# Splitting the even mixer's input weights during the first feed-forward instead of in the mixer

## The chip, the core and the metric

One core of a Trainium2 chip. The metric is the device time of one execution in microseconds (us). The engines are TensorE (PE, matmuls), VectorE (DVE), ScalarE (ACT), GpSimd (POOL) and SyncE (SP, which here only issues loads). SP and POOL can both issue DMA transfers; every engine takes its instructions strictly in order.

## The reference

Two layers over 256 latent and 256 context tokens of width 1024, all in float32. Layer 0 is what matters here:

```python
y = modulate(h, g, m[off], m[off + 1])                       # rmsnorm, scale, shift
h = h + 0.5 * m[off + 2] * swiglu(y, w_gu, w_down)           # half_ffn, context and latent
...
z_ctx = y_ctx @ w_in                                         # even_mixer: 1024 -> 2816
z_lat = y_lat @ w_in
f_lat = fourier_mix(z_lat[..., D_A_IN:])
r_l, v_l, kk_l, g_l, dirs_l = rwkv_features(token_shift(zA_lat, mu), *fargs)
S, y = wkv_scan(S0, ...)                                     # two directions, 12 heads
out = jnp.concatenate([o, f], axis=-1) @ w_out
```

The modulation vectors m come from c @ ada_w, a matrix-vector product of 1024 by 9216.

## The kernel before

**Products of float32 in three passes.** A weight tile of 128 columns (1024x128, 512 KB) is loaded by SP into a buffer `wraw` (4 of them). ACT casts it to the reduced format (`whi`, L190), DVE subtracts the cast from the original (`wlo`, L191), and `mm3` (L195 to L197) adds up whi·xh, whi·xl and wlo·xh on PE. In the first feed-forward whi/wlo stand in five pairs of buffers, in the mixer in four; a pair is used about four tiles after it is made.

**The first feed-forward** (`ffn`, context and latent together, 512 columns) goes over 22 blocks f in three parts: f 0 to 7, 8 to 14, 15 to 21. Each f takes two weight tiles (gate and up); then ACT makes `sg` = silu(gate), DVE multiplies it into `hd`, ACT casts `hh`, DVE subtracts `hl`. After each part comes `down`, 8 steps k, on the part's hh and hl. The last two k of the last part are done for context first, then for latent.

**Background jobs.** `net.jobs` is a list of generators; `run_jobs(n)` takes n steps of the first unfinished one before each f and each k. Before the change the jobs are the 28 `ada_job`s: POOL loads 1 MB (`adaw`, 3 buffers `ada0`), and DVE forms products with the conditioning row, with a scratch tile `adaj` (1 buffer), L281.

**The transition.** The last sums of squares go through DVE (`ms`, L347), POOL (a power, `rs`, L350) and PE (L356, spreads it over rows). DVE makes `hn`, ACT `yh` and DVE `yl` tile by tile k; POOL writes `hlat` to memory (`spill`, L1205). PE starts four weight tiles of the mixer at once, context columns first (v = 1), then latent (v = 0).

**The mixer's input part.** 22 weight tiles `win`, in the order of `win_order` (one, then six times three, then three). The first four are split at the end of the feed-forward; `even_in` splits each of the other 18 as it comes. Between them stand the `features` of the first group: token shift (`zp`, `z`), scans, the small products L631, L650 and the inverse of a triangular matrix (`Dt`, L678; L687). A scheduler that works with its own model of durations puts all instructions into each engine's order, so that a removed instruction can move others. The chain of scans follows from about 545 us on.

Of the kernel before, what the change touches and what calls it, by code (L numbers as in the profile page):

```python
# [7 lines left out]
F32 = mybir.dt.float32  # L8
F32R = mybir.dt.float32r
AF = mybir.ActivationFunctionType  # L10
ALU = mybir.AluOpType
AX = mybir.AxisListType

P = 128
D = 1024
KT = D // P
# [56 lines left out]
def win_order():  # L73
    o = [18]
    for j in range(NP):
        o += [NP + j, 2 * NP + j, j]
    return o + [19, 20, 21]
# [56 lines left out]
class Net:  # L134
# [138 lines left out]
    def ada_job(self, blk, vecs):  # L273
# [4 lines left out]
        for i in range(2):  # L278
# [3 lines left out]
                                               op1=ALU.mult, accum_out=self.mod[0, v][:, blk + i:blk + i + 1])  # L282
            yield

    def run_jobs(self, n):
        drive(self.jobs, n)

# [206 lines left out]
        self.bd = self.cst[:, C_BD:C_BD + P]  # L494

    def even_in(self, i, n, yh, yl):
        wh, wl = self.weight(self.ins["win"][i])
        tag = ("down", "mx", "down", "ada", "pg", "pg")[i % 6]
        if tag == "pg":
            if i % 2 == 0:  # L500
                self.two = self.bank("pg")
            ps = self.two[:, i % 2, :]
        else:
            ps = self.bank(tag)
        for k in range(KT):
            self.mm3(ps[:, :n], wh[:, k, :], wl[:, k, :], yh[:, k, :n], yl[:, k, :n], k == 0, k == KT - 1)
        return ps
# [601 lines left out]
def drive(gens, n):  # L1109

    while gens and n:
        if next(gens[0], gens) is gens:
            gens.pop(0)
        else:
            n -= 1


def body(tc, ins, out):
    with ExitStack() as ctx:
        nc = tc.nc  # L1120
        net = Net(ctx, tc, ins, out)
        psum = lambda name: tc.tile_pool(name=name, bufs=1, space=bass.MemoryType.PSUM)
        net.ada_setup()
        spill = tc.dram_tile([P, KT, T], F32, name="spill")
        acc = net.keep.tile([P, 2 * T], F32, name="acc")
        with ExitStack() as yp:
            ypool = yp.enter_context(tc.tile_pool(name="ey", bufs=1))
# [2 lines left out]
            op = ctx.enter_context(ExitStack())  # L1130
            mx = ExitStack()
            with tc.tile_pool(name="hc", bufs=1, side="right") as hcp, tc.tile_pool(name="f1", bufs=1) as fp:
                hc = hcp.tile([P, KT, T], F32, name="hctx")
                hl = hcp.tile([P, KT, T], F32, name="hlat")
                for q in range(4):
                    k = slice(2 * q, 2 * q + 2)
                    nc.sync.dma_start(hl[:, k, :], ins["tok"][0][:, k, :])
                    nc.sync.dma_start(hc[:, k, :], ins["tok"][1][:, k, :])
                h = [hl, hc]
                with psum("ps1") as net.pp:  # L1140
                    net.ap, net.hp = fp, ((ypool, 4),) * 4 + ((fp, 1),)
                    two = [fp.tile([P, 2, KT, 256], F32, tag=t, name="ada0" + t, bufs=1) for t in ("hh", "hl")]
                    load = [two[b // 2][:, b % 2] for b in range(4)]
                    load += [fp.tile([P, KT, 256], F32, tag="ada0", name=f"ada0{b}", bufs=3) for b in range(4, 7)]
                    load += [fp.tile([P, KT, 256], F32, tag="cb", name="ada07", bufs=1)]
                    nc.sync.dma_start(load[0], ins["ada0"][0])
                    srcs = [ins["gu"][0, f, j] for f in range(2) for j in range(2)]
                    raws = [net.load(x) for x in srcs]
                    for b in range(1, KT):
                        nc.sync.dma_start(load[b], ins["ada0"][b])  # L1150
                    yh, yl = parts2()
                    abt = fp.tile([P, 2, 2, KT], F32, name="ab0")
                    ab = [(abt[:, v, 1, :], abt[:, v, 0, :]) for v in range(2)]

                    def start():

                        first, ws = [], []

                        def begin(b):
                            if b < KT:  # L1160
                                first.append(net.ada_first(b, load[b], abt))
                                next(first[b])

                        def split():
                            ws.append(net.weight(srcs[len(ws)], 0, raws[len(ws)]))

                        def ready(k):
                            if k < KT:
                                drive([first[k]], 1)
                                net.modulate_tile(k, h, (0, 1), r, ab, yh, yl, fp)  # L1170

                        with tc.manual_schedule(engines={mybir.EngineType.PE, mybir.EngineType.DVE, mybir.EngineType.Activation}):
                            for k in range(KT):
                                for v in range(2):
                                    net.stat(acc, h[v][:, k, :], v, k)
                            rs = net.rates(net.sums(acc, (0, 1)), 4, D, NORM_EPS)
                            begin(0)
                            r = net.spread_rows(rs, 4)
                            for i in range(4):
                                if i == 1:  # L1180
                                    ready(0)
                                split()
                            begun = [net.bank("gu") for _ in ws]
                            for k in range(KT):
                                for n, (ps, (wh, wl)) in enumerate(zip(begun, ws)):
                                    net.mm3(ps, wh[:, k, :], wl[:, k, :], yh[:, k, :], yl[:, k, :], k == 0, k == KT - 1)
                                    if k and n == 0:
                                        ready(k + 1)
                                        if k == KT - 2:
                                            net.early = [net.weight(ins["gu"][0, 2, j], 0) for j in range(1)]  # L1190
                                if k == 0:
                                    begin(1)
                                    ready(1)
                                begin(k + 2)
                        return begun

                    net.jobs = [net.ada_rows_job(fp, (0, 1))]
                    net.jobs += [net.ada_job(m * KT + k, (0, 1) if m < 5 else (0,)) for m in range(2, 9) for k in range(0, KT, 2)]
                    gate = lambda: [net.modcol(0, v, 2, scale=0.5) for v in range(2)]
                    rate = {}  # L1200
                    net.between = net.rstd_steps(acc, 1, rate)
                    net.ffn(0, h, yh, yl, gate, acc, fp, 2, start)
                    net.run_jobs(100)
                ab = [(net.modcol(0, v, 4, g=net.normg(0, 1)), net.modcol(0, v, 3)) for v in range(2)]
                nc.gpsimd.dma_start(spill, hl)  # L1205
                yh, yl = parts2()
                net.pp = mx.enter_context(psum("pse"))
                net.even_params(net.keep)

                net.hp = ((ypool, 4),)  # L1210
                order = win_order()
                ws = [net.weight(ins["win"][i], 0) for i in range(4)]
                begun = [net.bank(t) for t in ("down", "down", "mx", "ada")]
                for v in (1, 0):
                    c = slice(v * T, v * T + T)
                    late = net.rstd_steps(acc, 0, rate) if v else None
                    for k in range(KT):
                        if v and k in (2, 5):
                            next(late)
                        net.modulate_tile(k, h, (v,), rate[v], ab, yh, yl, hcp)  # L1220
                        for m, ps, (wh, wl) in zip(order, begun, ws):
                            own = m < NP
                            if not (own and v):
                                net.mm3(ps[:, c], wh[:, k, :], wl[:, k, :], yh[:, k, c], yl[:, k, c],
                                        k == 0 and (own or v == 1), k == KT - 1, skip_group_check=True)
# [34 lines left out]
        with tc.tile_pool(name="late", bufs=1) as lp:  # L1260
            wide = [net.ada_wide(b, lp) for b in range(18)]
            outs = []
            for g in range(3):
# [7 lines left out]
                else:  # L1271
                    gate = net.modcol(0, 0, 5)
# [16 lines left out]
        h = [hl]  # L1289
# [3 lines left out]
        fp = ctx.enter_context(tc.tile_pool(name="post", bufs=1))  # L1293
# [72 lines left out]
```

## Time and profile before

| | |
|---|---|
| median of 3 runs | 1600.86 us (1598.47 to 1601.13) |
| the profiled execution | 1593.66 us, span in the trace 1592.0 us |
| busy in the span | PE 94%, DVE 68%, ACT 42%, POOL 13% |
| first feed-forward | to 404.8 us |
| mixer's input part with the first group's features | 404.8 to about 545 us |
| loads of `win` | 22 x 512 KB by SP, between 366.8 and 505.9 us |
| idle on POOL ahead of `rs` at 402.69 us | 194.86 us |

Shares are of the whole span. PE's busy time counts a matmul to its modelled end, so a stretch can be full while each matmul runs at half clock; the granted clock is a column of its own.

### The profile page before, as it was taken

What the parts mean: (1) busy time and instruction counts of PE and PEld (TensorE: products, weight loads), DVE (VectorE), ACT (ScalarE), POOL (GpSimd) and SP (SyncE); (2) the same over time, 40 slices, a digit from 0 to 9 for tenths busy, and PEclk for the clock granted to TensorE, in tenths of its full rate; (3) what the DMA queues carried; (4) which work ended last, traced back from release to release, by engine and by line L of the source; (5) the groups of instructions that cost most, each with busy time, mean ns of one, the idle gap of its engine ahead of it and who ended that gap; (6) DMA issues with size and microseconds to landing.
All of it is one profiled execution on the core that took longest, in us unless ns stands there. A gap on an engine that the chain in (4) does not pass through costs nothing.

```text
span 1592.0 us, 29925 instructions
## 1 busy us (share of the span) xinstructions
PE 1488.8 (94%) x12102; PEld 1279.8 (80%) x12102; DVE 1082.7 (68%) x1994; ACT 675.4 (42%) x1101; POOL 202.3 (13%) x293
## 2 busy tenths in 40 slices
PE   5999999999989979899998999999999986899997
PEld 3788888888877755455686999999999874899997
DVE  4799963334689699577266777657775399767753
ACT  3422222223454462542444555445554365445542
POOL 0000100000131151321211000000000075200000
PEclk9999999999999889999799999999999988899999
DMA  9676953232322025455432555655556432345562
GB/s 373 236 238 235 335 200 103 93 92 82 125 84 84 28 102 203 169 197 194 150 108 69 171 181 180 179 190 173 186 176 178 137 106 92 121 161 184 183 181 88
DMA packets 68810, 253.40 MB, mean 159 GB/s; under 512 B 8032, under 2 KB 10864, under 8 KB 63936
## 3 DMA queue, kind: packets, MB, share of 16 engines
q1 hardware_dynamic: 64080, 219.46, 42.0%
q0 software_dynamic: 4592, 32.03, 5.7%
q8 instruction: 95, 1.56, 0.4%
q14 instruction: 43, 0.35, 0.1%
HBM read 249.36 MB, written 2.10 MB: 158 GB/s over the span
## 4 chain that ended last, share of the span: by engine, by line
PE 80%; DVE 13%; ACT 2%; issue 2%; POOL 1%; DMA 1%; SPq 0%; POOLq 0%; DVEq 0%; ACTq 0%
PE gu L195 13%; PE gu L196 13%; PE gu L197 13%; PE down L195 7%; PE down L196 7%; PE down L197 7%; PE ada L260 3%; PE gu L970 1%; PE gu L1055 1%; DVE wlo L191 1%; DVE oo L1028 1%; DVE ocv L1028 1%; PE pg L746 1%; PE down L804 1%; PE misc L631 1%
## 5 line engine op out<-in xcount | busy, mean ns | idle before, releaser
L190 ACT CAST whi<-wraw 128x1024 fp32r<-128x1024 f32 (+1 forms) x298 | 304.6, 1026 | 524.1 <-PE gu L196 227.2
L191 DVE TENSOR_TENSOR wlo<-wraw,whi 128x1024 fp32r<-128x1024 f32 (+1 forms) x298 | 356.3, 1198 | 151.9 <-ACT whi L190 144.9
L195 PE MATMUL gu<-yh,whi 128*128 128x258 f32 (+1 forms) x1408 | 438.3, 312 | 6.2 <-ACT yh L375 4.3
L196 PE MATMUL gu<-yl,whi 128*128 128x258 f32 (+1 forms) x1408 | 437.7, 311 | 0.1
L197 PE MATMUL gu<-yh,wlo 128*128 128x258 f32 (+1 forms) x1408 | 436.8, 310 | 0.0
L195 PEld LDWEIGHTS gu<-yh,whi 128*128 128x128 f32 x1408 | 265.8, 189 | 24.1 <-ACT yh L375 5.7
L196 PEld LDWEIGHTS gu<-yl,whi 128*128 128x128 f32 x1408 | 267.2, 190 | 15.1 <-DVE yl L377 1.0
L197 PEld LDWEIGHTS gu<-yh,wlo 128*128 128x128 f32 x1408 | 267.3, 190 | 14.9 <-DVE wlo L191 0.8
L196 PE MATMUL down<-hl,whi 128*128 128x256 f32 (+1 forms) x704 | 217.3, 309 | 0.0
L195 PE MATMUL down<-hh,whi 128*128 128x256 f32 (+1 forms) x704 | 217.3, 309 | 0.0
L197 PE MATMUL down<-hh,wlo 128*128 128x256 f32 (+1 forms) x704 | 217.3, 309 | 0.0
L196 PEld LDWEIGHTS down<-hl,whi 128*128 128x128 f32 x704 | 134.4, 191 | 7.4
L195 PEld LDWEIGHTS down<-hh,whi 128*128 128x128 f32 x704 | 134.4, 191 | 7.4
L197 PEld LDWEIGHTS down<-hh,wlo 128*128 128x128 f32 x704 | 134.4, 191 | 7.4
L350 POOL TENSOR_TENSOR rs<-ms,mhalf 128x2 f32<-128x2 f32 (+1 forms) x9 | 10.9, 1208 | 821.4 <-DVE ms L347 821.4
L281 DVE SCALAR_TENSOR_TENSOR adaj<-adaw,cb 128x1024 f32<-128x1024 f32 x80 | 97.7, 1221 | 4.9 <-DMA adaw<-in_adat_dram 3.6
L260 PE MATMUL ada<-wraw,ccs 128*32 128x512 f32 x288 | 71.5, 625 | 0.7 <-DVE mod L269 0.7
L384 DVE SCALAR_TENSOR_TENSOR hlat<-down,mc,hlat 128x256 f32<-128x256 f32 x46 | 22.2, 483 | 63.0 <-PE down L197 63.0
L438 DVE COPY wb<-gu 128x1 f32<-128x1 f32 x132 | 20.2, 153 | 46.6 <-PE gu L197 46.6
L360 ACT CAST hh<-hd 128x256 fp32r<-128x256 f32 (+1 forms) x88 | 40.4, 461 | 25.0 <-DVE hd L433 14.2
L970 PE MATMUL gu<-yo,wraw 128*128 128x256 f32 x192 | 45.4, 396 | 1.9 <-ACT yo L375 1.9
L1012 POOL TENSOR_TENSOR opart<-opart,opr 128x256 f32<-128x256 f32 x54 | 44.9, 832 | 5.0 <-ACT opr L1010 1.2
(341 smaller groups left out, 2311.9 us busy)
## 6 DMA issues: line engine op xcount, KB each, us to landing
wraw<-in_gu_dram SPq DMA_DIRECT2D x176, 512.0 KB, 4.0
wraw<-in_ada_dram SPq DMA_DIRECT2D x72, 512.0 KB, 4.3
adaw<-in_adat_dram POOLq DMA_DIRECT2D x28, 1024.0 KB, 5.6
wraw<-in_down_dram SPq DMA_DIRECT2D x64, 448.0 KB, 3.3
wraw<-in_down_dram SPq DMA_DIRECT2D x32, 512.0 KB, 3.5
wraw<-in_win_dram SPq DMA_DIRECT2D x22, 512.0 KB, 3.8
wraw<-in_owin_dram SPq DMA_DIRECT2D x14, 512.0 KB, 3.6
ada<-in_ada_dram SPq DMA_DIRECT2D x4, 1024.0 KB, 16.8
```

Source lines behind the costliest of these rows:

```text
L190: nc.scalar.copy(hi[:, :k, :], raw[:, :k, :])
L191: (eng or nc.vector).tensor_tensor(out=lo[:, :k, :], in0=raw[:, :k, :], in1=hi[:, :k, :].bitcast(F32), op=ALU.subtract)
L195: mm(ps, lhsT=wh, rhs=xh, start=start, stop=False, **k)
L196: mm(ps, lhsT=wh, rhs=xl, start=False, stop=False, **k)
L197: mm(ps, lhsT=wl, rhs=xh, start=False, stop=stop, **k)
L260: nc.tensor.matmul(ps[32 * g:32 * g + 32, :], lhsT=self.cs[:, k, :], rhs=w[:, i, :], start=k < 4, stop=k >= 4, tile_position=(0, 32 * g), ...
L281: nc.vector.scalar_tensor_tensor(out=junk, in0=w[:, i, :], scalar=1.0, in1=self.cb[v], op0=ALU.mult, op1=ALU.mult, accum_out=self.mod[0, v ...
L360: self.nc.scalar.copy(hi, x)
L384: nc.vector.scalar_tensor_tensor(out=h[v][:, k, :], in0=ps[:, n * T:n * T + T], scalar=gate[v][:, k:k + 1], in1=h[v][:, k, :], op0=ALU.mul ...
L970: nc.tensor.matmul(ps[:, :n], lhsT=w[:, k, :], rhs=y[:, k, :], start=k == 0, stop=k == KT - 1)
L1012: nc.gpsimd.tensor_tensor(out=part, in0=prev, in1=pr, op=ALU.add)
L1028: nc.vector.scalar_tensor_tensor(out=c, in0=u[:, w:w + T], scalar=cw[:, j, w:w + 1], in1=c, op0=ALU.mult, op1=ALU.add)
```

## The change

Each of the 22 tiles of `win` gets a job, behind the 28 `ada_job`s: POOL loads the raw tile into the scratch tile `adaj` (1 buffer, the same that the ada products used), ACT casts it, DVE subtracts, and POOL writes both results (1 MB) to a tensor `halves[i]` in memory. The steps per f and per k go from 2 to 3. In the mixer `ready_weight` takes the place of `weight`: SP loads whi and wlo (512 KB each) straight into the pair's buffers. So 44 loads (22 MB) by SP stand where 22 (11 MB) stood, POOL issues 22 loads (11 MB) and 22 writes (22 MB) more, and the 22 casts and 22 subtractions move from the mixer and the feed-forward's end into the feed-forward.

```diff
--- before.py
+++ after.py
@@ -281,6 +281,28 @@
                 nc.vector.scalar_tensor_tensor(out=junk, in0=w[:, i, :], scalar=1.0, in1=self.cb[v], op0=ALU.mult,
                                                op1=ALU.mult, accum_out=self.mod[0, v][:, blk + i:blk + i + 1])
             yield
+
+    def halves_job(self, i):
+
+        nc = self.nc
+        raw = self.ap.tile([P, KT, P], F32, tag="adaj", name=self.nm("adaj"), bufs=1)
+        nc.gpsimd.dma_start(raw, self.ins["win"][i])
+        yield
+        w = self.ap.tile([P, 2, KT, P], F32R, tag="ada0", name=self.nm("halves"), bufs=3)
+        nc.scalar.copy(w[:, 0], raw)
+        nc.vector.tensor_tensor(out=w[:, 1], in0=raw, in1=w[:, 0].bitcast(F32), op=ALU.subtract)
+        nc.gpsimd.dma_start(self.halves[i], w.bitcast(F32))
+        yield
+
+    def ready_weight(self, i):
+
+        pool, bufs = self.hp[self.turn % len(self.hp)]
+        self.turn += 1
+        hi = pool.tile([P, KT, P], F32R, tag="whi", name=self.nm("whi"), bufs=bufs)
+        lo = pool.tile([P, KT, P], F32R, tag="wlo", name=self.nm("wlo"), bufs=bufs)
+        for q, t in enumerate((hi, lo)):
+            self.nc.sync.dma_start(t.bitcast(F32), self.halves[i][:, q])
+        return hi, lo
 
     def run_jobs(self, n):
         drive(self.jobs, n)
@@ -494,7 +516,7 @@
         self.bd = self.cst[:, C_BD:C_BD + P]
 
     def even_in(self, i, n, yh, yl):
-        wh, wl = self.weight(self.ins["win"][i])
+        wh, wl = self.ready_weight(i)
         tag = ("down", "mx", "down", "ada", "pg", "pg")[i % 6]
         if tag == "pg":
             if i % 2 == 0:
@@ -1122,6 +1144,7 @@
         psum = lambda name: tc.tile_pool(name=name, bufs=1, space=bass.MemoryType.PSUM)
         net.ada_setup()
         spill = tc.dram_tile([P, KT, T], F32, name="spill")
+        net.halves = [tc.dram_tile([P, 2, KT, P], F32, name=f"halves{i}") for i in range(len(win_order()))]
         acc = net.keep.tile([P, 2 * T], F32, name="acc")
         with ExitStack() as yp:
             ypool = yp.enter_context(tc.tile_pool(name="ey", bufs=1))
@@ -1196,10 +1219,11 @@
 
                     net.jobs = [net.ada_rows_job(fp, (0, 1))]
                     net.jobs += [net.ada_job(m * KT + k, (0, 1) if m < 5 else (0,)) for m in range(2, 9) for k in range(0, KT, 2)]
+                    net.jobs += [net.halves_job(i) for i in range(len(win_order()))]
                     gate = lambda: [net.modcol(0, v, 2, scale=0.5) for v in range(2)]
                     rate = {}
                     net.between = net.rstd_steps(acc, 1, rate)
-                    net.ffn(0, h, yh, yl, gate, acc, fp, 2, start)
+                    net.ffn(0, h, yh, yl, gate, acc, fp, 3, start)
                     net.run_jobs(100)
                 ab = [(net.modcol(0, v, 4, g=net.normg(0, 1)), net.modcol(0, v, 3)) for v in range(2)]
                 nc.gpsimd.dma_start(spill, hl)
@@ -1209,7 +1233,7 @@
 
                 net.hp = ((ypool, 4),)
                 order = win_order()
-                ws = [net.weight(ins["win"][i], 0) for i in range(4)]
+                ws = [net.ready_weight(i) for i in range(4)]
                 begun = [net.bank(t) for t in ("down", "down", "mx", "ada")]
                 for v in (1, 0):
                     c = slice(v * T, v * T + T)
```

POOL's order from the end of the feed-forward on, before: the last `adaw` loads, then `rs` of the context half, the write of `hlat`, `rs` of the latent half.

```order
L277 DMA adaw_373_2043<-in_adat_dram 128x2048
L277 DMA adaw_380_2079<-in_adat_dram 128x2048
L350 TENSOR_TENSOR rs_513_2937<-ms_512_2935,mhalf_68 128x2
L587 MEMSET ff_591_3399 128x8
L1205 DMA spill_80<-hlat_92 128x2048
L350 TENSOR_TENSOR rs_543_3057<-ms_542_3055,mhalf_68 128x2
```

After the change (`adaj` as the target of a load is a raw tile of `win`; `halvesN` on the left is tile N in memory, `halves` on the right its two parts in SBUF):

```order
L289 DMA adaj_441_2351<-in_win_dram 128x1024
L294 DMA halves19_100<-halves_452_2421 128x2048
L289 DMA adaj_453_2425<-in_win_dram 128x1024
L294 DMA halves20_101<-halves_454_2427 128x2048
L289 DMA adaj_465_2499<-in_win_dram 128x1024
L372 TENSOR_TENSOR rs_557_3091<-ms_556_3089,mhalf_68 128x2
L1229 DMA spill_80<-hlat_114 128x2048
L294 DMA halves21_102<-halves_466_2501 128x2048
L372 TENSOR_TENSOR rs_583_3203<-ms_582_3201,mhalf_68 128x2
```

The write of tile 20 and the load of raw tile 21 now stand ahead of the context half's `rs`, and the write of tile 21 ahead of the latent half's; in front of these rows the 38 others alternate in the same way from the last `adaw` on.

ACT's order at the end of part 2 of the feed-forward, before (the last `sg` and `hh` here are those of f = 14):

```order
L432 ACTIVATE sg_321_1777<-gu_316_1721 128x512
L190 CAST whi_356_1942<-wraw_358_1944 128x896
L360 CAST hh_243_1337<-hd_322_1778 128x512
L190 CAST whi_363_1978<-wraw_365_1980 128x896
L432 ACTIVATE sg_334_1851<-gu_329_1795 128x512
L190 CAST whi_370_2014<-wraw_372_2016 128x896
L360 CAST hh_243_1337<-hd_335_1852 128x512
L190 CAST whi_377_2050<-wraw_379_2052 128x896
```

And with the change, the same place:

```order
L454 ACTIVATE sg_351_1865<-gu_346_1809 128x512
L190 CAST whi_386_2042<-wraw_388_2044 128x896
L382 CAST hh_267_1407<-hd_352_1866 128x512
L292 CAST halves_354_1873<-adaj_353_1871 128x1024
L190 CAST whi_393_2080<-wraw_395_2082 128x896
L454 ACTIVATE sg_364_1941<-gu_359_1885 128x512
L190 CAST whi_400_2120<-wraw_402_2122 128x896
L382 CAST hh_267_1407<-hd_365_1942 128x512
L292 CAST halves_368_1953<-adaj_355_1877 128x1024
L190 CAST whi_407_2158<-wraw_409_2160 128x896
```

The casts of tiles 3 and 4 stand around the `sg` and `hh` of f = 14, so that these come behind the arrival of raw tile 3. The other casts stand in the same way, one in two or three of ACT's weight casts; that of tile 20 stands four rows ahead of the mixer's first `yh`, that of tile 21 between the second `yh` and the third.

SP's order at the transition, before:

```order
L181 DMA wraw_504_2849<-in_down_dram 128x896
L181 DMA wraw_525_2998<-in_win_dram 128x1024
L181 DMA wraw_528_3004<-in_win_dram 128x1024
L181 DMA wraw_531_3010<-in_win_dram 128x1024
L181 DMA wraw_534_3016<-in_win_dram 128x1024
L181 DMA wraw_584_3354<-in_win_dram 128x1024
L181 DMA wraw_607_3453<-in_win_dram 128x1024
L181 DMA wraw_613_3494<-in_win_dram 128x1024
L547 DMA up_573_3322<-in_up_dram 128x256
L845 DMA gup_1238_6917<-in_gup_dram 128x128
```

And with the change:

```order
L304 DMA whi_571_3158<-halves2_83 128x1024
L304 DMA wlo_572_3159<-halves2_83 128x1024
L304 DMA whi_573_3162<-halves3_84 128x1024
L304 DMA wlo_574_3163<-halves3_84 128x1024
L569 DMA up_613_3468<-in_up_dram 128x256
L867 DMA gup_1260_7027<-in_gup_dram 128x128
L569 DMA up_653_3669<-in_up_dram 128x256
L304 DMA whi_622_3498<-halves4_85 128x1024
L304 DMA wlo_623_3499<-halves4_85 128x1024
L304 DMA whi_644_3595<-halves5_86 128x1024
L304 DMA wlo_645_3596<-halves5_86 128x1024
```

Before, raw tiles 4, 5 and 6 are asked for ahead of `up`, and wait only for a `wraw`. Now the parts of tile 4 come behind both `up` loads, and their targets are the pair of buffers that tile 0 holds until its last matmul.

## Rows read from the trace of the kernel before

**Rows 1.** The page: busy time, share, instructions.

```profile
PE 1488.8 (94%) x12102; PEld 1279.8 (80%) x12102; DVE 1082.7 (68%) x1994; ACT 675.4 (42%) x1101; POOL 202.3 (13%) x293
```

**Rows 2.** Windows: length, busy by engine, PE clock, DMA share, GB/s.

```profile
100.00:220.00 120.00, 120.00 (x523) 97.90 (x522) 114.23 (x195) 30.99 (x36) 11.09 (x21) 1.00 0.77 276
220.00:400.00 180.00, 180.00 (x810) 147.97 (x809) 68.32 (x96) 48.52 (x67) 0.00 (x0) 1.00 0.30 95
428.00:545.00 117.00, 106.24 (x1017) 90.70 (x1016) 97.99 (x166) 59.96 (x88) 24.28 (x49) 0.91 0.26 84
```

**Rows 3.** Groups of instructions by line, 428 to 530 us.

```profile
L191 DVE TENSOR_TENSOR wlo<-wraw,whi 128x1024 fp32r<-128x1024 f32 x18 | 22.1, 1244 | 6.8 <-PE ada L196 6.4 <-ACT whi L190 0.3
L190 ACT CAST whi<-wraw 128x1024 fp32r<-128x1024 f32 x18 | 18.4, 1045 | 23.4 <-PE down L196 12.5 <-PE pg L196 8.3 <-PE ada L196 2.5
```

**Rows 4.** PE's waits, 428 to 545 us: total, times, longest.

```profile
PE misc L631 <- POOL zp L514: 3.9, 2, 3.4
PE misc L650 <- DVE bk L604: 2.5, 1, 2.5
PE misc L687 <- DVE Dt L678: 1.8, 1, 1.8
```

**Rows 5.** Timeline of all engines, 402 to 411 us: the transition.

```profile
402.45 0.16 DVE L347 TENSOR_SCALAR ms<-misc 128x2 f32<-128x2 f32 x1 [0.30 <-PE misc L335]
...
405.02 0.48 DVE L384 SCALAR_TENSOR_TENSOR hlat<-gu,mc,hlat 128x256 f32<-128x256 f32 x1 [0.83 <-PE gu L197]
...
405.80 0.59 POOL L1205 DMA_DIRECT2D spill<-hlat  x1 [0.59 <-DVE hlat L384]
...
406.71 0.50 PE L195 MATMUL down<-yh,whi 128*128 128x256 f32 x2 [1.52 <-ACT yh L375]
...
410.58 0.48 PE L195 MATMUL down<-yh,whi 128*128 128x256 f32 x2
```

**Rows 6.** The tile `cb`: its two loads (512 KB each), and their landings.

```profile
L239 POOL DMA_DIRECT2D cb<-in_crow_dram x2: 527/528/530, 54.3 to 54.8; - x2
...
DMA to landing us min/median/max: 4.3/4.7/5.0
```

**Rows 7.** DMA issues of POOL, 60 to 410 us: KB, median to landing.

```profile
spill<-hlat POOLq DMA_DIRECT2D x1, 1024.0 KB, 5.5
```

**Rows 8.** The same, 68 to 140 us.

```profile
adaw<-in_adat_dram POOLq DMA_DIRECT2D x10, 1024.0 KB, 5.1
```

**Rows 9.** The same, 192 to 209 us.

```profile
adaw<-in_adat_dram POOLq DMA_DIRECT2D x4, 1024.0 KB, 7.9
```

**Rows 10.** Timeline of DVE around the last ada product.

```profile
216.86 1.21 DVE L281 SCALAR_TENSOR_TENSOR adaj<-adaw,cb 128x1024 f32<-128x1024 f32 x1
```

**Rows 11.** Timeline, 249 to 253.6 us: the last block f of part 2.

```profile
250.02 0.62 ACT L360 CAST hh<-hd 128x512 fp32r<-128x512 f32 x1
...
253.23 0.39 PE L195 MATMUL down<-hh,whi 128*128 128x512 f32 x1
253.47 0.40 PE L196 MATMUL down<-hl,whi 128*128 128x512 f32 x1
```

**Rows 12.** Timeline of PE, 468 to 474 us: behind its longest wait.

```profile
469.03 1.98 PE L631 MATMUL misc<-cst,inv 128*64 128x128 f32 x16 [3.42 <-POOL zp L514]
...
472.39 0.63 PE L196 MATMUL pg<-yl,whi 128*128 128x512 f32 x1
472.81 0.63 PE L197 MATMUL pg<-yh,wlo 128*128 128x512 f32 x1
```

**Rows 13.** Timeline, 427 to 431 us: the first `even_in` tile.

```profile
427.66 0.28 PE L197 MATMUL down<-yh,wlo 128*128 128x256 f32 x1
...
428.96 0.50 PE L195 MATMUL pg<-yh,whi 128*128 128x512 f32 x1
...
430.22 0.50 PE L197 MATMUL pg<-yh,wlo 128*128 128x512 f32 x1 [0.53 <-DVE wlo L191]
```

**Rows 14.** The tensor `win`: landings of its 22 loads.

```profile
DMA to landing us min/median/max: 3.2/3.8/5.9
```

## The prediction

> **What bounds the kernel now.** The page comes first: PE is busy 94% of the span [rows 1], so only what PE waits for counts. The windows then split the stretch that the change touches in three [rows 2]. From 100 to 220 us PE is full (120.00 of 120) and DVE nearly so (114.23, mostly ada products). From 220 to 400 us PE is full again (180.00 of 180) while DVE does 68 us, ACT 49 and POOL nothing, and the DMA engines are busy 0.30 of the time: this is the empty room into which the jobs are put. From 428 to 545 us, the mixer's input part, PE does 106.24 of 117 us at a mean granted clock of 0.91 while DVE does 98. There 18 subtractions take 22.1 us of DVE and 18 casts 18.4 us of ACT [rows 3], and PE's three longest kinds of wait (8.2 of its 10.8 idle us) are on the features: L631 behind `zp`, L650 behind `bk`, L687 behind `Dt` [rows 4]. So the change takes work from a stretch where DVE makes PE wait and puts it where PE never waits. What it adds is latency: a chain of jobs, and a first wait of PE for loads.
>
> **The chain of jobs.** All 22 raw tiles go through `adaj`, of which there is one buffer. A raw load is issued behind the write of the tile before it, and its cast and subtraction must read it before the next may land. So one tile costs a cycle c = cast + subtraction + step to POOL + write and load. Cast 1.05, subtraction 1.24 [rows 3]; latencies on the way about 0.1; the step from DVE's end to POOL's issue, 0.3, is that from `hlat` (ends 405.50) to the write (405.80) [rows 5]. Write and load stand in no row together. Lower bound: the load overtakes the write, then only POOL's issue of the write (0.59 [rows 5]) stands before a load that lands as the two of `cb` did, 4.7 [rows 6]: 5.3. In turn: the one write of 1 MB landed 5.5 after its issue [rows 7], and of the two `cb` loads, issued 0.5 apart and landed after 4.3 and 5.0 (I read the later as the slower), the second came 1.2 behind the first [rows 6]: 6.7. Upper bound: four 1 MB loads that followed each other closely needed 7.9 where those of a quieter stretch needed 5.1 [rows 8, 9]; 7.9 behind the issue of the write is 8.5. I take 6.5, near the value in turn, because both go through one queue. So c = 9.2, between 8.0 and 11.2.
>
> The Trainium skill, "DMA: Bandwidth & Descriptors", section "Two DMAs through the same engine are not ordered", says that descriptors of one queue start in order but are pipelined; the 1.2 us between the `cb` loads agrees, and by it the load would not overtake. Its section "Anatomy of one DMA" prices a GpSimd transfer at 2.0 us plus its bytes at 436 GB/s, an estimate of 5.6 us for write and load in a row; the landings of `cb` (4.3 to 5.0 for 512 KB) lie above its 3.2.
>
> The first raw load must wait for the last ada product, which ends at 218.07 [rows 10]: issued 218.4, landed about 222.9. Cast i then comes at 222.9 + c·i, tile 20 at 406.9. Behind its subtraction (done 409.2) DVE has the last updates of `hlat` and `ms`, about 0.5, so `ms` stands at 409.7 instead of 402.45. From `ms` to the mixer's first matmul were 4.26 us (402.45 to 406.71 [rows 5]); POOL's two issues, ahead of `rs`, add 0.7 (0.3 and two times 0.59 against 0.65 for `hlat` and `ms`). PE starts the mixer at 414.7 instead of 406.71: 8.0 late. Tile 21's raw lands at 416.1, its subtraction ends at 418.4, and `yl` of k = 2 stands behind it, 418.9; PE asked for k = 2 3.9 us after its first matmul [rows 5], 418.6. That adds 0.3 to 0.5. Together D = 8.5, and 2.0 more or less for each 0.1 of c. It cannot go below about 2, since the subtraction of tile 20 (1.24) and the two issues (1.2) stand ahead of `rs` even when the chain keeps pace; that is so below c = 8.8, where cast 20 would have come at 398.9.
>
> Part of D shows earlier, and isn't added. ACT takes its casts in order, so that a late raw tile holds `hh` behind it. Cast 3 comes at 250.5; behind it stand a weight cast, `sg`, another and `hh`, some 3.7 us with the 1.05: `hh` is ready at 254.2, where before it was at 250.64 and PE asked for it at 253.23 [rows 11]. PE stalls there 1 to 2 us, and again at the end of part 3. The weight casts themselves have the lead of several buffers and are covered.
>
> **The clock.** Behind a wait of 3.42 us, PE still did matmuls of 512 columns every 0.42 us at 472.81, where elsewhere they come every 0.24 [rows 11, 12]: the lower of its two levels, 1.2 instead of 2.4 GHz, for 3.8 us or more from 469.03, of which half is lost, 1.9 or more. A start of the mixer 8 us late, of which most is one wait, I charge with 2.5, by that row a little longer; nothing, if the lateness is cut into short waits.
>
> **The first even_in.** Before, its raw tile lay ready, and PE waited 0.53 for the subtraction [rows 13]. Now its two parts go into the buffers of tile 0, whose last matmul ends at 427.94 [rows 13]. SP's loads of `win` landed after 3.2 to 5.9, median 3.8 [rows 14]: whi is there at 431.3 to 431.8, wlo a little later. PE began this tile at 428.96. So it waits 2.4 to 3.5 more, less the 0.53: 2.5. Queued behind on PE is the whole rest of the input part. Later pairs of loads have the time of a whole tile on PE (24 matmuls at 0.23 are 5.6 us for those with 512 columns) plus the lead of three other pairs, and cost nothing; without that lead each would cost the same 2.5. `up` waits for the write of tile 21 (about 424), is ahead of these loads on SP, and lands before 427.9 plus D; hidden by the context and latent halves of the first four tiles, 21 us.
>
> **More traffic.** 22 loads and writes, 34.6 MB in 180 us, are 192 GB/s beside 95: the level of 100 to 220 us, 276 GB/s at a share of 0.77, where PE didn't wait [rows 2]. I charge nothing beyond c; if SP's weight loads came too late all the same, each us would count on PE in full. Three job steps instead of two add no work and DVE was full there already: nothing, at worst a product ahead of a needed subtraction (1.2).
>
> **The gain.** 22.1 us leave DVE's 98 in the input part [rows 2, 3]. At best all 10.8 idle us go and the clock's 9% of 117 with them, 18 after what both share; at worst nothing, since the scheduler also moves the features' matmuls earlier in PE's order, so that they may be waited for as long. The three waits of 8.2 [rows 4] are on chains through DVE. I let three quarters of them go, 6, and with the longest the slow stretch behind it, 2 to 3: 9.
>
> **Sum.** 8.5 + 2.5 + 2.5 - 9 = +4.5. The profiled execution took 1593.7, which is 7.2 below the median of the runs shown (and below all three); 1598.2 in its terms is 1605 beside a median of 1600.9. A difference under 0.2%, 3.2 us, can't be told from no change.
>
> **The rivals.**
> *The chain keeps pace (faster).* If write and load overlap, c is near 8.0 to 8.6 and D is 2. No wait is then long enough to slow the clock: 2 + 2.5 - 9 = -4.5, 1596. For it: the lower bound. Against it: one queue, and the two `cb` loads. It decides below c = 9.0, where the sum is nil. By the formula of the Trainium skill, "DMA: Bandwidth & Descriptors", "Anatomy of one DMA", the estimate of 5.6 us would make c 8.3 and this the outcome.
> *The chain falls far behind.* Contention with SP's loads and the wait for DVE or ACT between other work make c 9.7 or more: D = 18 at 9.7, 25 at 10. +14 to +21: 1615 to 1622. For it: 7.9 us for close 1 MB loads, and a DMA share of about 0.8. Against: those had two megabytes in flight. The upper bound itself, 11.2, would be 40 us on top of the forecast and is left out of the range for that reason.
> *No relief in the mixer.* PE waits for the features as before, only in other places: the gain is 0 to 2 with D as forecast, about 1613. For it: the bound is latency through POOL, ACT and DVE, not DVE's load alone (L631 waits for POOL's `zp`). Against: DVE does 98 of 117 us there.
>
> **How the numbers follow.** Forecast (c 9.0 to 9.5, gain 6 to 12; 1601 to 1610): 0.42, of it 0.13 within 0.2% and 0.29 slower. Pace kept: 0.26 (0.24 faster, 0.02 same). Far behind: 0.18, slower. No relief: 0.14 (0.05 same if c is small, 0.09 slower). So faster 0.24, same 0.20, slower 0.56. The range from 1595 to 1619 leaves out the slower half of the second rival and the best of the first; the forecast's own is 1601 to 1610.
>
> **What would show it.** POOL's raw loads at even distances: 9.2 or not. ACT waiting for `adaj` ahead of its half casts; PE idle for `hh` about 253 us and 6 us or more ahead of the mixer's first matmul, with a lower clock behind it; a wait of about 3 us of the first pg matmul on a load; DVE at some 76 us in the input part, and PE's waits for `zp`, `bk` and `Dt` shorter. The prediction is wrong above all if c is off by 0.3, which moves the time by 6 us, or if the slow clock follows the late start for longer than it did in the row.

## The result, and the profile after

The changed kernel took 1610.74 us (median of 6 runs, 1608.81 to 1615.55) beside 1599.99 us for the kernel before; the ratio is 1.0070, with a 95% interval from 1.0055 to 1.0086. It is slower by 10.7 us, 8.8 to 13.8. The forecast was slower, 1605 in a range from 1595 to 1619: the sign and the range held, and the 4.5 us of its sum are less than half of what came. The profiled executions are 1593.66 before and 1608.81 after, 15 us apart; the one of before lies 6 us below its own median, and a second profile of each kernel (below) shows how much of the traces is chance.

The windows of the changed kernel stand beside those of [rows 2]: length, busy time by engine (PE, PE's weight loads, DVE, ACT, POOL), PE's clock, DMA share, GB/s.

```profile
220.00:260.00 40.00, 40.00 (x177) 32.79 (x176) 18.68 (x23) 14.90 (x18) 4.24 (x8) 1.00 0.72 255
...
340.00:380.00 40.00, 35.88 (x150) 28.64 (x149) 16.92 (x20) 14.83 (x20) 4.24 (x8) 0.96 0.66 236
380.00:420.00 40.00, 34.67 (x194) 29.97 (x193) 19.76 (x39) 11.07 (x21) 5.55 (x10) 0.96 0.79 273
...
443.71:556.70 112.99, 103.39 (x1011) 87.06 (x1011) 74.84 (x146) 40.62 (x67) 22.90 (x47) 0.94 0.48 163
```

The feed-forward, full on PE before, has holes from 340 us on. The last window is the mixer's input part, which now begins at 443.71 instead of 428.96: DVE has 75 us of work instead of 98, and yet the part is only 3.3 us shorter (116.3 from 428.96 to 545.27 before, 113.0 now).

The timeline of POOL shows the chain of jobs (start, duration, line, what, idle before and what ended it):

```profile
212.60 0.53 POOL L289 DMA_DIRECT2D adaj<-in_win_dram  x1 [10.35 <-DVE mc L314]
218.91 0.54 POOL L294 DMA_DIRECT2D halves<-halves  x1 [5.78 <-DVE halves L293]
219.43 0.54 POOL L289 DMA_DIRECT2D adaj<-in_win_dram  x1
...
390.51 0.54 POOL L294 DMA_DIRECT2D halves<-halves  x1 [8.06 <-DVE halves L293]
391.04 0.53 POOL L289 DMA_DIRECT2D adaj<-in_win_dram  x1
403.14 0.54 POOL L294 DMA_DIRECT2D halves<-halves  x1 [11.57 <-DVE halves L293]
403.67 0.53 POOL L289 DMA_DIRECT2D adaj<-in_win_dram  x1
413.59 0.54 POOL L294 DMA_DIRECT2D halves<-halves  x1 [9.39 <-DVE halves L293]
414.12 0.53 POOL L289 DMA_DIRECT2D adaj<-in_win_dram  x1
414.66 0.74 POOL L372 TENSOR_TENSOR rs<-ms,mhalf 128x2 f32<-128x2 f32 x1
```

From the write of tile 0 to that of tile 18 there are 171.60 us, 9.53 per tile: eleven cycles of 9.1 to 9.3 us and seven of 10.1 to 10.3, in which the cast begins about 7 us after its load's issue instead of 6 (why was not found). The next two cycles take 12.6 and 10.5: by then, from 390.57 us on, SP loads the first ready parts. The DMA share of 0.79 by itself does not explain it, since it was 0.82 from 260 to 300 us at cycles of 9.1 to 9.2. The `rs` that the mixer waits for stands right behind the write of tile 20 and the load of raw tile 21.

PE's waits in the changed kernel, 55 to 560 us (total, times, longest), are:

```profile
PE down L195 <- ACT hh L382: 3.9, 1, 3.9
PE misc L653 <- POOL inv L584: 3.1, 2, 2.8
PE misc L357 <- ACT sq L336: 3.0, 1, 3.0
PE pg L195 <- DMA whi<-halves: 2.7, 1, 2.7
PE pg L195 <- DVE z L540: 2.6, 2, 2.3
PE misc L709 <- DVE Dt L700: 1.3, 1, 1.3
```

Of [rows 4], the waits of L631 (now L653) and of L687 (now L709) are still there, shorter, the first now for `inv`; that for `z` is 2.6 instead of 0.9. The first, third and fourth are the price of the change. ACT's timeline shows how the first comes about:

```profile
369.64 1.04 ACT L292 CAST halves<-adaj 128x1024 fp32r<-128x1024 f32 x1 [6.33 <-DMA adaj<-in_win_dram]
370.59 0.93 ACT L190 CAST whi<-wraw 128x896 fp32r<-128x896 f32 x1
...
372.57 0.62 ACT L382 CAST hh<-hd 128x512 fp32r<-128x512 f32 x1 [1.05 <-DVE hd L455]
```

ACT stands idle for 6.3 us before a raw tile that has not landed, and the last `hh` of part 3 comes behind it, too late for PE. Over 220 to 400 us ACT waits 63.4 us in 16 such places:

```profile
ACT halves L292 <- DMA adaj<-in_win_dram: 63.4, 16, 7.7
```

At the transition it goes on, now with the sums of squares that `rs` needs (timeline of all engines):

```profile
410.99 1.04 ACT L292 CAST halves<-adaj 128x1024 fp32r<-128x1024 f32 x1 [5.15 <-DMA adaj<-in_win_dram]
411.94 0.41 ACT L336 ACTIVATE sq<-hctx 128x256 f32<-128x256 f32 x1
...
412.40 0.38 PE L357 MATMUL misc<-cst,sq 128*128 128x1 f32 x2 [3.04 <-ACT sq L336]
```

The mixer's first matmul (406.71 in [rows 5]) and the first `even_in` ([rows 13]) stand in PE's timeline as:

```profile
418.48 0.52 PE L195 MATMUL down<-yh,whi 128*128 128x256 f32 x2 [1.11 <-ACT yh L397]
...
443.71 0.50 PE L195 MATMUL pg<-yh,whi 128*128 128x512 f32 x1 [2.67 <-DMA whi<-halves]
...
445.00 0.79 PE L197 MATMUL pg<-yh,wlo 128*128 128x512 f32 x1 [0.55 <-DMA wlo<-halves]
445.59 0.63 PE L195 MATMUL pg<-yh,whi 128*128 128x512 f32 x1
```

So the mixer starts 11.8 us late, the first `even_in` is 14.7 us late, and a matmul of 512 columns there takes 0.63 instead of the 0.40 that [rows 11] show: behind the wait PE is at the lower of its two clock levels.

### The profile page after: what moved, and what is told of

It is laid out like the page before. It is cut to its first block, busy times and chain, and to the rows that moved or that the text cites. A ratio compares the mean times of both kernels' runs of the same rounds, so it can differ in the third digit from the quotient of the medians.

```text
span 1607.1 us, 30067 instructions
## 1 busy us (share of the span) xinstructions
PE 1494.6 (93%) x12102; PEld 1280.5 (80%) x12102; DVE 1080.4 (67%) x1994; ACT 676.1 (42%) x1101; POOL 223.8 (14%) x337
## 4 chain that ended last, share of the span: by engine, by line
PE 72%; DVE 14%; DMA 6%; ACT 3%; issue 3%; POOL 1%; SPq 0%; POOLq 0%; DVEq 0%; ACTq 0%
PE gu L195 12%; PE gu L196 12%; PE gu L197 12%; PE down L196 6%; PE down L195 6%; PE down L197 6%; DMA adaj<-in_win_dram 4%; PE ada L260 3%; DVE ocv L1050 1%; DVE oo L1050 1%; PE gu L1077 1%; PE pg L768 1%; PE down L826 1%; DVE halves L293 1%; PE down L806 1%
## 5 line engine op out<-in xcount | busy, mean ns | idle before, releaser
L190 ACT CAST whi<-wraw 128x1024 fp32r<-128x1024 f32 (+1 forms) x276 | 281.8, 1024 | 400.7 <-PE gu L196 157.6
L191 DVE TENSOR_TENSOR wlo<-wraw,whi 128x1024 fp32r<-128x1024 f32 (+1 forms) x276 | 329.3, 1195 | 114.9 <-ACT whi L190 114.7
L197 PEld LDWEIGHTS gu<-yh,wlo 128*128 128x128 f32 x1408 | 267.6, 190 | 14.7 <-DVE wlo L191 0.5
L293 DVE TENSOR_TENSOR halves<-adaj,halves 128x1024 fp32r<-128x1024 f32 x22 | 27.0, 1226 | 82.3 <-ACT halves L292 82.3
L292 ACT CAST halves<-adaj 128x1024 fp32r<-128x1024 f32 x22 | 23.1, 1049 | 87.3 <-DMA adaj<-in_win_dram 77.4
```

The source lines that it names most:

```text
L190: nc.scalar.copy(hi[:, :k, :], raw[:, :k, :])
L191: (eng or nc.vector).tensor_tensor(out=lo[:, :k, :], in0=raw[:, :k, :], in1=hi[:, :k, :].bitcast(F32), op=ALU.subtract)
L197: mm(ps, lhsT=wl, rhs=xh, start=False, stop=stop, **k)
L292: nc.scalar.copy(w[:, 0], raw)
L293: nc.vector.tensor_tensor(out=w[:, 1], in0=raw, in1=w[:, 0].bitcast(F32), op=ALU.subtract)
```

## Experiments

All times are medians beside runs of the kernel before on the same chip; ratios carry a 95% interval.

**The jobs alone.** The mixer goes back to splitting its own raw tiles:

```diff
-                ws = [net.ready_weight(i) for i in range(4)]
+                ws = [net.weight(ins["win"][i], 0) for i in range(4)]
...
-        wh, wl = self.ready_weight(i)
+        wh, wl = self.weight(self.ins["win"][i])
```

> The 22 jobs run as in the change, but the mixer loads and splits its raw tiles as before. If the lateness comes from the chain of jobs (theory): the mixer's first matmul is 10 to 12 us late, nothing is won or lost behind it, 1610 to 1612 us beside 1600. If it comes from the loads of the ready parts (rival): 1600 to 1602.

Measured: 1612.0, ratio 1.0062 (1.0046 to 1.0079). In its trace the mixer's first matmul stands at 417.52, 10.8 late, behind a wait of 4.8 us for `hh` at the end of part 3 and one of 3.0 for `yh`. This is the theory's time, and the lateness comes from the chain, without any ready load. The last two cycles of the chain take 9.2 us each here, so that the 12.6 and 10.5 of the changed kernel belong to its ready loads.

**The cycle without the write.** The same, with the write of the parts left out as well:

> The 22 jobs of the change without the write of the parts to memory; the mixer loads and splits as before. It shows the cycle without the write. If load and write go through their queue in turn: 7.0 to 7.5 us per tile instead of 9.5. If the load does not wait for the write: 9 us.

POOL's raw loads (timeline: the first and the last of the 22) and the landing of raw tiles (the view of the tile `adaj`, min, median, max), here:

```profile
212.51 0.53 POOL L289 DMA_DIRECT2D adaj<-in_win_dram  x1 [11.15 <-DVE mc L313]
...
346.71 0.53 POOL L289 DMA_DIRECT2D adaj<-in_win_dram  x1 [5.69 <-DVE halves L293]
```

```profile
DMA to landing us min/median/max: 3.4/3.7/4.2
```

and the same view of the changed kernel:

```profile
DMA to landing us min/median/max: 3.7/6.0/9.4
```

6.39 us per tile (134.20 by 21) instead of 9.53. A raw load behind the write lands 2.3 us later than one without it. So the load does not pass the write, as forecast; whether it waits its turn in the queue or shares the DMA engines with the write, this run does not separate. The load alone is quicker than the 4.7 of `cb` [rows 6], which is why the cycle is below the expected 7.0. The kernel took 1605.7 (one time). Its mixer starts at 410.95, 4.2 late, although its last cast comes at 350.7: PE waits 2.1 us for `hctx` in the feed-forward.

**Ready loads without a chain.** One job; the first four tiles as before; the other 18 load the parts of tile 0 in place of their own, with the same instructions, and the job steps are two again. A second run leaves the first `even_in` as before too, so that 17 tiles are loaded ready:

```diff
-                    net.jobs += [net.halves_job(i) for i in range(len(win_order()))]
+                    net.jobs += [net.halves_job(i) for i in range(1)]
...
-            self.nc.sync.dma_start(t.bitcast(F32), self.halves[i][:, q])
+            self.nc.sync.dma_start(t.bitcast(F32), self.halves[0][:, q])
...
-        wh, wl = self.ready_weight(i)
+        wh, wl = self.weight(self.ins["win"][i]) if i < 5 else self.ready_weight(i)   # 17 tiles only
```

> One job only, two steps per block as before; the first four tiles are split as before; the other 18 load both parts of tile 0 (so the mixer computes with the wrong weights, with the same instructions). It shows what the mixer wins without any lateness ahead of it. Theory (the relief is the 3.3 us read in the changed kernel's trace, the first even_in waits 2.7 us more): 1599 to 1600 us beside 1600. If the relief is the 9 us of the prediction and the late start hid it: 1593 to 1595.

> One job only; tiles 5 to 21 load both parts of tile 0 (wrong weights, the same instructions), the first even_in splits its tile as before. Beside the run with 18 such loads (1597) it shows what the first even_in's wait costs. Theory (2.7 us of wait and the slow clock behind it): 1591 to 1594. Rival (the wait costs only itself): 1594.5 to 1596.

Measured: with 18 ready tiles 1597.25, ratio 0.9978 (0.9963 to 0.9994); with 17, 1590.33, ratio 0.9950 (0.9930 to 0.9970). The first lies between its two expectations, the second just below the theory's. Windows from the first `even_in` to the chain of scans, with 18 and with 17:

```profile
432.11:545.07 112.96, 105.01 (x1010) 88.19 (x1010) 74.85 (x146) 40.65 (x67) 23.20 (x47) 0.91 0.47 164
```

```profile
428.50:536.40 107.90, 98.95 (x1011) 83.34 (x1010) 78.64 (x150) 43.01 (x71) 23.03 (x49) 0.98 0.49 174
```

The relief of the mixer is worth some 8 us (0.50% of 1599), near the 9 of the forecast, if nothing is late; the first `even_in` gives back 4.5 us of it by the ratios, whose intervals overlap, and 6.9 by the medians. Its wait is 2.64 us in the trace; the rest lies behind it, where the clock is lower. These are the first 15 us, with 18 and with 17:

```profile
432.11:447.10 14.99, 14.67 (x60) 11.18 (x61) 6.25 (x12) 5.77 (x10) 2.16 (x4) 0.68 0.68 251
```

```profile
428.50:443.50 15.00, 12.82 (x74) 10.10 (x74) 11.87 (x18) 9.31 (x16) 2.28 (x7) 1.00 0.84 316
```

In all six traces with this wait the clock of these 15 us is below 1.00 (0.68, 0.77 and four times 0.89), in all four with 17 ready tiles it is 1.00. In the rest of the part the clock differs between the runs too; why was not found.

**Fewer tiles.** The change itself for tiles 5 to 21 only, the first five as before:

> Jobs and ready loads only for tiles 5 to 21; the first four and the first even_in as before. Theory: the chain ends some 48 us earlier, no lateness, no wait of the first even_in, the relief of 3 us stays: 1596 to 1598 us. Rival (the mixer wins nothing): 1600.

Measured: 1597.95, ratio 0.9988 (0.9972 to 1.0004). In its trace the last write is issued at 372.08, and yet PE waits 4.1 us for `hh` at the end of part 3 and the mixer starts at 413.49, 6.8 late. So the expectation of no lateness failed: not the end of the chain makes PE late there, but a cast that stands ahead of `hh` in ACT's order. The time is in the theory's range all the same, since the relief is larger than the 3 us it assumed. In the changed kernel the end of the chain comes later still (11.8), and hides this stall.

**More buffers.** The raw tile is loaded into the place of its low part, in the three buffers of the ada weights:

```diff
-        raw = self.ap.tile([P, KT, P], F32, tag="adaj", name=self.nm("adaj"), bufs=1)
-        nc.gpsimd.dma_start(raw, self.ins["win"][i])
-        yield
         w = self.ap.tile([P, 2, KT, P], F32R, tag="ada0", name=self.nm("halves"), bufs=3)
+        raw = w[:, 1].bitcast(F32)
+        nc.gpsimd.dma_start(raw, self.ins["win"][i])
+        yield
```

> All 22 jobs, but the raw tile is loaded into the place of its low part, in the three buffers of the ada weights, so that three loads can be on their way. Theory (one raw buffer makes the chain serial at 9.5 us per tile, and this is the lateness): the chain keeps pace, the first matmul of the mixer is 2 to 3 us late, 1600 to 1603 us. Rival (34.6 MB more traffic makes loads late whatever the buffers): 1607 us or more.

Two more runs ask for each load two tiles ahead of its cast, and let the generator pass one tile per block f or step k (three yields per tile instead of two), with 22 and with 17 tiles:

> All 22 jobs in the three buffers of the ada weights, but paced: one tile per block f or step k, and each raw load issued two tiles ahead of its cast. Theory (the cost in the feed-forward is ACT, in order, standing before a raw tile that has not landed, not the traffic as such): no wait for hh, the mixer's first matmul 0 to 2 us late; what stays is the relief of the mixer less the wait of the first even_in: 1597 to 1600 us beside 1600. Rival (34.6 MB more traffic delays the weight loads however it is spread): 1604 or more.

> The same pacing for tiles 5 to 21 only, the first four and the first even_in as before. Theory: no lateness, no wait of the first even_in, the relief of some 8 us that the run with 17 tiles showed from the first even_in to the chain: 1591 to 1594 us. Rival (the relief there was an accident of the clock): 1597 to 1600.

Measured: in place 1605.79, ratio 1.0039 (1.0025 to 1.0052); paced, 22 tiles, 1611.89, ratio 1.0086 (1.0062 to 1.0109); paced, 17 tiles, 1604.6, ratio 1.0038 (1.0023 to 1.0054). All three miss the theory's time: in place lies between theory and rival, paced with 22 in the rival's range, paced with 17 above both. The windows of the paced run with 17 tiles show why:

```profile
220.00:312.00 92.00, 79.89 (x329) 62.85 (x328) 42.02 (x51) 31.75 (x36) 14.38 (x28) 0.93 0.91 336
```

```profile
PE down L195 <- ACT hh L393: 10.0, 2, 7.5
```

The pace was not kept: the scheduler pulled casts and transfers to the front, the last write was issued at 312 us, and the DMA engines were busy 0.91 of the time. ACT met raw tiles that had not landed again (52.2 us in 12 places), and PE waited 10.0 us for `hh`. In place, the stall reaches PE through DVE: a subtraction waits 8.6 us for its cast, with `hctx` behind it, and PE waits 7.6 us for `hctx`. By these runs alone the rival, traffic, would have stood.

**The casts in program order.** The paced kernels, with one call more:

```diff
-            nc.scalar.copy(w[:, 0], raw)
+            self.tc.keep_in_program_order(nc.scalar.copy(w[:, 0], raw))
```

> As the paced run with 22 tiles, but ACT's casts of the halves keep the program's order, one per block f or step k, so that the scheduler cannot pull them to the front of the feed-forward (in the paced runs it did: a tile every 6 us, DMA engines busy 0.9 of the time, ACT waiting for raw tiles ahead of hh). Theory (ACT standing before raw tiles is the cost): waits for hh of a microsecond at most, the mixer's first matmul 0 to 2 us late, 1597 to 1600 us beside 1600. Rival (the traffic itself): 1604 or more.

> The same for tiles 5 to 21, with the first four and the first even_in as before. Theory: nothing lost in the feed-forward and the relief of the run that only loaded 17 tiles (1590): 1590 to 1594 us. Rival (the traffic itself): 1598 or more.

Measured: 22 tiles 1595.71, ratio 0.9979 (0.9961 to 0.9997); 17 tiles 1589.24, ratio 0.9937 (0.9917 to 0.9958), the fastest of all and faster than both kernels. The windows, 22 tiles and 17 tiles:

```profile
220.00:400.00 180.00, 180.00 (x809) 147.98 (x808) 90.56 (x114) 67.79 (x87) 21.80 (x41) 1.00 0.79 284
```

```profile
220.00:400.00 180.00, 180.00 (x809) 147.96 (x809) 86.61 (x111) 64.76 (x84) 16.55 (x31) 1.00 0.66 234
```

PE is full again, with 22 tiles at a DMA share of 0.79. The mixer starts at 406.43 and 406.69. ACT, with 22 tiles:

```profile
ACT halves L302 <- DMA halves<-in_win_dram: 22.6, 7, 7.1
```

ACT still stands before raw tiles, but for 22.6 us instead of 63.4, and PE no longer waits for an `hh`. So the same bytes and the same casts cost PE nothing in the feed-forward when no `hh` that it needs stands behind a raw tile on its way; the rival as it was put, however the traffic is spread, falls. Both times are a little below the theory's. The kept order also spread the traffic: a raw tile lands after 6.2 us (median) instead of the 8.3 of the paced run with 22. How much of the cure is the order itself and how much the quicker landing is not separated.

**Second profiles of both kernels.**

> The kernel before, unchanged, for a second profile of it. The input part (first even_in to the chain of scans) took 116.3 us there, the rest to the end 1046.7; the two runs whose mixer is as before took 115 to 116 and 1054. If the first profile was a lucky one: 115 to 117 us and 1050 to 1055 here. If the kernels with ready parts win nothing behind the chain's start: 1046 to 1048.

> The changed kernel, unchanged, for a second profile of it beside the kernel before on the same chip: 1610 us. The cycle of the chain 9.5 us, the mixer's first matmul at 417 to 420 us and the wait of the first even_in 2.6 to 2.7 us should come again, since no clock enters them; the slow stretches behind that wait and at 596 to 617 us need not.

Measured: before 1599.37, ratio 0.9997 (0.9977 to 1.0016); changed 1610.86, ratio 1.0066 (1.0046 to 1.0086). In the second trace of the kernel before, the input part took 115.0 us and the rest 1053.8, so that its first profile was a lucky one. In that of the changed kernel the cycle is 9.54 up to tile 18 and then 12.1 twice, the first matmul at 423.15 (outside the 417 to 420 expected), the first `even_in` waits 2.72.

## Why the prediction came out as it did

**Right: what is bound by what.** The serial chain through one raw buffer, load behind write, was the main cost, and it made the mixer late. Write and load were put at 6.5 us; from the write's issue to the raw tile's landing they are 6.5 in the trace (0.53 and the median of 6.0), and the cycle is 9.53 beside 9.2. The rule of the Trainium skill, "DMA: Bandwidth & Descriptors", section "Two DMAs through the same engine are not ordered", that descriptors of one queue start in order, agrees with the 2.3 us that a load loses behind a write; a sharing of the engines would agree with them too. The estimate of 5.6 us by the Trainium skill, "DMA: Bandwidth & Descriptors", section "Anatomy of one DMA", is 0.9 too small here, and with it the rival that the chain keeps pace.

**Near by luck: the lateness.** The sum had 8.5 for D and 2.5 for the clock behind it. The first matmul is 11.8 late (16.6 in the second trace). The step that failed is "Cast i then comes at 222.9 + c·i" with an even c of 9.2. Cast 0 came at 216.31, 6.6 early: the last ada product starts at 211.1 with three job steps instead of 216.86, and the first raw tile landed sooner. The next 18 cycles took 171.6 us instead of 165.6, 6.0 more. The two behind them took 23.1 instead of 18.4, 4.7 more, and the run of the jobs alone, where they take 9.2 each, puts that down to the ready loads. Together cast 20 came at 410.99 instead of 406.9; from it to the first matmul there are 7.5 us, as forecast (7.8). With the start that was forecast and the cycles that came, the mixer would have been some 19 us late (8.0 and 10.7): an unforeseen early start made up for most of a c that was too small.

The clock charge of 2.5 did not come there. From the first matmul to the first `even_in` the trace has 25.2 us instead of 22.2, and its two waits (0.6 and 2.7, where 0.5 was before) explain that at a clock of 1.00. The slow stretches are ahead, 0.96 from 340 to 420 us, where the chain and not PE sets the start of the mixer: PE waits 3.0 and 1.1 us just ahead of it. The jobs alone cost 0.62%, 9.9 us, near the 11 of the sum.

**Wrong in place: the stall at part 2.** No wait came about 253 us (40.00 of 40): cast 3 came at 244.66 instead of 250.5, and `hh` was not late. The stall at the end of part 3 came, 3.9 us.

**Mis-sized most: the first even_in.** 2.5 was forecast, and the wait itself is 2.7 (2.67 and 0.55, less the 0.53 before). But it costs 4.5 to 6.9 us, as the pair of runs with 18 and 17 ready tiles shows, and the pair with kept casts again (0.9979 and 0.9937, 6.7 us, with intervals that do not overlap). A clock charge belonged here: at 0.89 to 0.68 the first 15 us behind the wait lose 1.7 to 4.8 us, an estimate from their length and clock.

**The gain: right in size, not by the step that was given.** 9 was forecast, of it 6 from PE's waits for the features. 17 ready tiles without lateness gave 0.50%, 8 us, and, with the jobs, 0.63%. But the idle time of PE in the input part hardly fell: some 10.7 us before, 8 to 9.6 with ready tiles. As in the third rival, PE waits for the features in other places instead (`z`, `inv`); that the size came out all the same is luck. From the first `even_in` to the end, the four traces whose mixer splits its tiles have 1163 to 1171 us, six with 18 ready tiles 1159 to 1165, and four with 17 1156 to 1161. In the input part alone they have 115 to 116, 112 to 114 and 108 to 115, at clocks from 0.91 to 0.98. So only 1 to 3 us of the gain are idle time in the input part; how the rest divides between PE's clock there and what follows stays open.

**The sum again.** 11.8 late, 4.5 to 6.9 for the first `even_in` and 8 won give 8 to 11, beside the 10.7 that were measured. The estimate leaves out what differs by chance behind the input part.

**The rivals.** *Chain far behind* (1615 to 1622) had c of 9.7 or more by contention with SP's loads, and over the 20 cycles that count c is 9.73: its condition came true, and the early start kept its price away. *No relief* has the waits right and the time wrong; the runs without a chain speak against its price. *Traffic*, charged with nothing, cost PE nothing by itself: the Trainium skill, "DMA: Bandwidth & Descriptors", section "Issuing engines are not separate DMA queues", says that transfers of all issuing engines run on the same 16 DMA engines, and at a share of 0.79 PE did not wait in the run with kept casts. At 0.9, in the paced runs, it did, through ACT; that a weight load of SP came late there was not seen. On the chain the ready loads did cost, 4.7 us.

## What to carry to other kernels

Work put into the idle time of an in-order engine is free only while its operand is there: a cast that waits for a load holds everything queued behind it, and idle time of an engine off the path says nothing about that. When a scheduler is free to move such work, fix its place in the consumer's queue and ask for the load well ahead; more buffers alone moved it forward here and left the kernel 0.39% slower than before, instead of 0.70%. Count the first tile after a change of supply separately, with the slow clock behind its wait.

## What was unexpected of the hardware

The same stretch of program, from the chain's start to the first L829 (L851), took 59.77 us in the first profile of the kernel before and 64.32 in the second, with the same busy time of DVE and ACT; what differs is PE's clock, and with it PE's busy time:

```profile
545.27:605.04 59.77, 50.53 (x758) 34.10 (x758) 51.26 (x94) 33.46 (x62) 26.82 (x40) 0.91 0.27 94
```

```profile
543.82:608.14 64.32, 55.63 (x759) 37.63 (x758) 50.93 (x94) 33.52 (x62) 26.85 (x40) 0.81 0.25 88
```

The changed kernel has both too, 63.75 at 0.84 in its first profile and 59.48 at 0.94 in its second. So a stretch full of short waits differs by 4 to 5 us between executions of one kernel, as much as the terms that were predicted here; what decides it was not found.
